# A four-layer trunk: the MLP's input at other offsets, logits in other ticks, a rebuilt start

## The chip, the cores and the metric

The kernel is one launch on one core of a Trainium2 chip. The metric is device time in microseconds (us), taken as the median of several executions. Five engines matter here: PE (TensorE) multiplies matrices and transposes, ACT (ScalarE) and DVE (VectorE) work elementwise, POOL (GpSimd) does small work, SP (SyncE) issues DMAs. They run side by side and meet through semaphores. SBUF is the on-chip memory that PE reads; PSUM has eight banks per partition that PE writes.

## The reference, cut to what matters

```python
D_MODEL, SEQ, DEPTH, D_FF = 1024, 256, 4, 4096     # batch 1, float32
for i in range(DEPTH):
    kind = i % 3            # 0 retention (layers 0 and 3), 1 MoBA attention, 2 differential attention
    h = rmsnorm(x, norm1[i])
    x = x + mixer[kind](h)  # retention: 4 heads, q and k of 256 with rotary, v and gate of 512
                            # attention: 16 heads of 64, q and k normed per head, a T5 bias added
    x = x + square(relu(rmsnorm(x, norm2[i]) @ w_up[i])) @ w_down[i]
return x
```

At 256 tokens the MoBA layer has one block only, so it is plain causal attention. Layers 0 and 3 are retention, layer 1 is MoBA, layer 2 is differential attention.

## The kernel before, in words

**Three passes.** Every float32 operand of a large product is cut in two parts: hi (rounded to the matmul's input format, made by an ACT copy) and lo (the rest, made by a DVE subtraction). `passes` (L310 to L313) then makes three matmuls: hi times hi (L311), one mixed (L312), the other mixed (L313). The activations' parts are `xhi`, `xlo`, the weights' are `whi`, `wlo`.

**Weights.** They stream through SBUF: SP loads `raw` tiles of 1 MB (three buffers) by `load_raw`, each tile is cut into two pieces, `split_piece` (ACT, L173) and `split_lo` (DVE, L183) make the two parts of a piece; `advance` does so up to four pieces ahead of the matmuls, `take` hands a piece out. A matmul takes one operand as "weights", loaded into the array ahead of it (PEld), and streams the other one, the "moving" one. In `mm_a` (q and k of retention: tile `qk`; the MLP's first product: tile `up`) the model weights are loaded and the activations move, 256 columns at a time. In `mm_b` (`vg`, `qkv`) and `mm_o` (`acc`) the activations are loaded and the model weights move, 512 columns at a time.

**Offsets.** `hi_lo` (L86) gives `wlo` a pad of 32 or 96 floats, by the piece's parity, and by whether the piece is narrow (256 columns wide). `norm_new` (L271) lays out `xhi` and `xlo` with pads of 80 and 48 floats, and shifts them for the MLP. What counts in this case is the address modulo 512 bytes: all `whi` lie at 160; `wlo` lies at 32 for narrow pieces and at 160 for wide ones; the MLP's `xhi` lies at 96 and `xlo` at 352, any other `xhi` and `xlo` at 160. While one matmul streams its moving operand, the next one's weights are loaded. Moving minus loaded is thus 448, 320, 448 bytes in the three passes of `up`, and 0, 128, 0 in those of `qk`.

**Order.** The order on each engine is that of the code. A clock counts ticks: `tick` comes after each step of a large product, `later(n, f)` queues a step for n ticks on, and steps due in the same tick go by the table `ORDER` (L64), the transposes of q and k (`qk_t`) late in it.

**Attention.** Layers 1 and 2 make q, k (two halves `b` of 8 heads each) and v in six blocks of four `mm_b`, one tick each. `qk_t` transposes a half to `qT`, `kT` (PE, then ACT copies), `softmax` (L632) makes logits of one pair of heads (PE, tile `sc`, two PSUM banks), adds the bias and takes the maximum (DVE, L651), and exponentiates (ACT, L654); `probs`, `probs_t` and `av_moba` or `av_diff` follow a few ticks later. V is copied from PSUM by ACT (L761, tile `vt`); `av_moba` (tile `oT`) and `av_diff` (tile `od`) need it. Four auxiliary PSUM banks go round among `sc`, `pT`, `qkT`, `oT`, `od`, `up`, `qk`. The table `SM0` (L590) sets the ticks of the softmaxes of the half b = 0 (12 to 15) and of b = 1 (20, 20, 21, 21); k of the half b = 1 is transposed in tick 19.

**Start.** X comes in four transfers of 256 KB, the first weights in two halves, `cos`, `sin` and the decay tables (`kd`, L427) in one transfer that ACT issues. `norm_quarter` (L280) transposes X and makes `xhi` and `xlo` a half of the features at a time; the first 1/rms (`rms`, L295) follows three ticks later.

Of the kernel before, what the change touches and what calls it, by code (L numbers as in the profile page):

```python
# [31 lines left out]
def trunk(ctx, tc, x_in, rel_bias, norm1, norm2, w_up, w_down, ret_w_in, ret_w_out,  # L32
# [108 lines left out]
    raws, pieces = {}, {}  # L141
    nxt = [0, 0, 0, 0]

    def load_raw(half=None):
        i = nxt[0]
        if i >= len(specs):
            return
        src, a, b = specs[i]
        if half != 1:
            raws[i] = rp.tile([P, a, b], F32, tag="raw", name="raw", bufs=NRAW)  # L150
        if half is None:
            nc.sync.dma_start(raws[i], src)
        else:
            hs = slice(half * (a // 2), (half + 1) * (a // 2))
            nc.sync.dma_start(raws[i][:, hs, :], src[:, hs, :])
        if half != 0:
# [68 lines left out]
    POOL.dma_start(rows2[0:32, :], norm2.rearrange("l (c p) -> (l c) p", p=P))
    for i, w in enumerate((moba_q_norm, moba_k_norm, diff_q_norm, diff_k_norm)):
        for g in range(2):
            POOL.dma_start(rows2[32 + i:33 + i, g * HD:(g + 1) * HD], w)
    POOL.dma_start(rows2[36:37, :], diff_subln)
# [193 lines left out]

    def retention(l):
        OT = {}
        kd = mp.tile([P, 8, S], F32, tag="kd", name="kd")
        ACT.dma_start(kd[:, 0:6, :], c_rd.rearrange("a p s -> p a s"))  # L427
        cos_b = kd[:, 0:1, :].to_broadcast([P, 2, S])
        sin_b = kd[:, 1:2, :].to_broadcast([P, 2, S])

# [140 lines left out]
    def attention(l):  # L571
# [8 lines left out]
        def at(tk, fn, *a):  # L580
            later(max(t0 + 1 + tk - clock[0], 0), fn, *a)
# [189 lines left out]
    for t in range(2):
        norm_quarter(0, 0, 0, t)
    split_piece()
    split_lo()
    for t in range(2):
        later(1, norm_quarter, 0, 0, 1, t)
    later(1, split_piece)
    later(1, split_lo)
# [51 lines left out]
```

## Time and profile before

| | |
|---|---|
| median of 3 executions | 1351.65 us (1350.81 to 1352.14) |
| the profiled execution's own time | 1352.26 us |
| its span, first to last instruction | 1350.4 us |
| mean granted TensorE clock | 0.998 |
| PE, DVE, ACT, POOL busy | 99%, 62%, 51%, 8% of the span |
| DMA | 242.27 MB, mean 179 GB/s |
| chain that ended last | PE 97%, ACT 1%, DMA 1% |

A time line row gives the start in us from the span's first instruction, the duration, the engine and line, the tiles, and in brackets how long the engine was idle before and what released it. Matmuls overlap: a row's duration runs to the modelled end of the matmul, so the pace of PE is read from the differences of starts.

### The profile page before, as it was taken

The page shows a single profiled execution, that of the slowest core. Times are in us where ns is not written, and L with a number is a line of the kernel's source. Part 1 is how long each engine was busy: PE and PEld are TensorE (multiplying, and loading weights), DVE is VectorE, ACT ScalarE, POOL GpSimd, SP SyncE. Part 2 cuts the span into 40 slices and gives each one's busy share as a digit, 9 for nine tenths or more (in the row PEclk, how much of TensorE's full clock was granted, in tenths as well). Part 3 has the DMA queues.
Part 4 walks back from the last instruction along what each step waited for, and adds up shares of the span by engine and source line. Part 5 has one row for each costly group of instructions (what it writes and reads, how often), then busy time and mean ns, then how long its engine had stood idle before and what let it go on. Part 6 is the DMA issues. An engine that isn't in the chain of part 4 may idle for free.

```text
span 1350.4 us, 19806 instructions
## 1 busy us (share of the span) xinstructions
PE 1333.6 (99%) x8020; PEld 1170.5 (87%) x8020; DVE 840.6 (62%) x1238; ACT 689.3 (51%) x1063; POOL 106.6 (8%) x314
## 2 busy tenths in 40 slices
PE   7999999999999999999999999999999999999998
PEld 6888889999987779999987789999988888899997
DVE  6766647555568856555578576555667675565554
ACT  5544446444456746444466754444455444554442
POOL 3111100000022000000021110000031011000000
PEclk9999999999999999999999999999999999999999
DMA  8545455555565336555554346555564555465551
GB/s 275 182 162 176 167 196 180 188 187 191 194 210 187 125 125 222 188 188 187 188 176 135 125 140 230 193 187 187 177 205 143 185 171 187 149 225 198 194 187 63
DMA packets 140797, 242.27 MB, mean 179 GB/s; under 512 B 4256, under 2 KB 87920, under 8 KB 140704
## 3 DMA queue, kind: packets, MB, share of 16 engines
q1 hardware_dynamic: 137872, 236.99, 52.3%
q0 software_dynamic: 1072, 2.35, 0.6%
q10 hardware_dynamic: 1760, 1.66, 0.4%
q8 instruction: 63, 1.03, 0.3%
q14 instruction: 30, 0.25, 0.1%
HBM read 239.91 MB, written 1.07 MB: 178 GB/s over the span
## 4 chain that ended last, share of the span: by engine, by line
PE 97%; ACT 1%; DMA 1%; DVE 0%; issue 0%; SPq 0%; ACTq 0%; DVEq 0%
PE acc L311 12%; PE acc L312 12%; PE acc L313 12%; PE up L312 9%; PE up L313 9%; PE up L311 9%; PE vg L311 4%; PE vg L313 4%; PE vg L312 4%; PE qkv L311 3%; PE qkv L313 3%; PE qkv L312 3%; PE qk L313 2%; PE qk L311 2%; PE qk L312 2%; PE xt L286 1%
## 5 line engine op out<-in xcount | busy, mean ns | idle before, releaser
L183 DVE TENSOR_TENSOR wlo<-raw,whi 128x1024 fp32r<-128x1024 f32 (+1 forms) x449 | 529.4, 1219 | 107.9 <-ACT whi L173 100.1
L173 ACT ACTIVATE whi<-raw 128x1024 fp32r<-128x1024 f32 (+1 forms) x449 | 451.8, 1051 | 89.7 <-PE acc L313 66.4
L311 PE MATMUL up<-xhi,whi 128*128 128x256 f32 x1024 | 283.8, 277 | 0.0
L312 PE MATMUL up<-xlo,whi 128*128 128x256 f32 x1024 | 283.5, 277 | 0.0
L313 PE MATMUL up<-xhi,wlo 128*128 128x256 f32 x1024 | 283.2, 277 | 0.0
L311 PE MATMUL acc<-whi,uu 128*128 128x512 f32 x512 | 199.9, 391 | 0.0
L312 PE MATMUL acc<-wlo,uu 128*128 128x512 f32 x512 | 199.6, 390 | 0.0
L313 PE MATMUL acc<-whi,uu 128*128 128x512 f32 x512 | 199.5, 390 | 0.0
L312 PEld LDWEIGHTS up<-xlo,whi 128*128 128x128 f32 x1024 | 192.3, 188 | 2.2
L311 PEld LDWEIGHTS up<-xhi,whi 128*128 128x128 f32 x1024 | 192.2, 188 | 2.2
L313 PEld LDWEIGHTS up<-xhi,wlo 128*128 128x128 f32 x1024 | 192.5, 188 | 0.0
L392 DVE SCALAR_TENSOR_TENSOR u<-up,u 128x512 f32<-128x512 f32 x64 | 44.2, 691 | 203.7 <-ACT u L391 203.5
L391 ACT ACTIVATE u<-up 128x512 f32<-128x512 f32 x64 | 38.1, 595 | 240.9 <-PE up L313 240.9
L313 PEld LDWEIGHTS acc<-whi,uu 128*128 128x128 f32 x512 | 96.1, 188 | 20.2
L311 PEld LDWEIGHTS acc<-whi,uu 128*128 128x128 f32 x512 | 96.1, 188 | 17.8
L312 PEld LDWEIGHTS acc<-wlo,uu 128*128 128x128 f32 x512 | 96.1, 188 | 17.7
L311 PE MATMUL vg<-whi,xhi 128*128 128x512 f32 x256 | 100.5, 393 | 0.0
L313 PE MATMUL vg<-whi,xlo 128*128 128x512 f32 x256 | 99.8, 390 | 0.0
L312 PE MATMUL vg<-wlo,xhi 128*128 128x512 f32 x256 | 99.7, 389 | 0.0
L311 PE MATMUL qkv<-whi,xhi 128*128 128x512 f32 x192 | 78.6, 409 | 0.0
L311 PE MATMUL acc<-whi,oh 128*128 128x512 f32 x192 | 76.5, 398 | 0.0
L313 PE MATMUL qkv<-whi,xlo 128*128 128x512 f32 x192 | 75.7, 394 | 0.0
(212 smaller groups left out, 1803.1 us busy)
## 6 DMA issues: line engine op xcount, KB each, us to landing
raw<-in_w_up_dram SPq DMA_DIRECT2D x64, 1024.0 KB, 5.6
raw<-in_w_down_dram SPq DMA_DIRECT2D x64, 1024.0 KB, 5.9
raw<-in_ret_w_in_dram SPq DMA_DIRECT2D x47, 1024.0 KB, 5.2
raw<-in_ret_w_out_dram SPq DMA_DIRECT2D x16, 1024.0 KB, 4.8
raw<-in_moba_w_in_dram SPq DMA_DIRECT2D x12, 1024.0 KB, 5.2
raw<-in_diff_w_in_dram SPq DMA_DIRECT2D x12, 1024.0 KB, 5.1
raw<-in_moba_w_out_dram SPq DMA_DIRECT2D x4, 1024.0 KB, 4.9
raw<-in_diff_w_out_dram SPq DMA_DIRECT2D x4, 1024.0 KB, 5.1
```

The source lines that it names most:

```text
L173: ACT.activation(hi[:, part], half[:, part], AF.Copy)
L183: DVE.tensor_tensor(lo[:, part], half[:, part], hi[:, part].bitcast(F32), op=OP.subtract)
L286: PE.transpose(ps[:, i * P:(i + 1) * P], X[:, t, k * P:(k + 1) * P], ident)
L311: PE.matmul(ps, lhsT=ah, rhs=bh, start=first, stop=False, skip_group_check=True)
L312: PE.matmul(ps, lhsT=ah, rhs=bl, start=False, stop=False, skip_group_check=True)
L313: PE.matmul(ps, lhsT=al, rhs=bh, start=False, stop=last, skip_group_check=True)
L391: ACT.activation(u, ps, AF.Relu)
L392: DVE.scalar_tensor_tensor(u, ps, 0.0, u, op0=OP.max, op1=OP.mult)
```

## The change

**Offsets.** `hi_lo` loses its pads, so every part of the weights lies at 160 modulo 512. `norm_new` shifts both parts of the MLP's input by one number of floats, `SHIFT`, that differs by layer: moving minus loaded weights is 448, 352, 320 and 192 bytes in layers 0, 1, 2 and 3, the same in all three passes. Other activations stay at 160, so all three passes of `qk` are at distance 0. The 512-column products keep their distance.

**Logits.** `SM0` lists a tick for each softmax. Those of b = 1 move from ticks 20, 20, 21, 21 to 19, 19, 20, 21, in layers 1 and 2. Two of the four thus follow the transposes of k directly.

**Start.** X comes in four column quarters, the first weights in parts of two k, alternating on SP, and `cos`, `sin` and the decay come on SP too. Nine matmuls on zeroed bf16 data (`hot`) stand ahead on PE. `first_qk` transposes, splits and multiplies two k at a time. POOL's small loads wait for tick 4, `head_weights` goes from tick 10 to 14. Pieces up to the fourth are split in two halves.

```diff
@@ hi_lo
-        n = a * b
-        hi = wp.tile([P, n], F32R, tag="hi", name="whi", bufs=NPC)
-        odd = i % 2
-        lo = wp.tile([P, n + (32 if odd else 96)], F32R, tag="lo%d" % (i % NPC), name="wlo", bufs=1)
-        o = 0 if odd == narrow else (32 if odd else 96)
-        return (t.rearrange("p (a b) -> p a b", a=a) for t in (hi, lo[:, o:o + n]))
+        return (wp.tile([P, a, b], F32R, tag=t, name="w" + t, bufs=NPC) for t in ("hi", "lo"))
@@ parts
-        m = n if i else n // 2
+        m = n if i > 3 else n // 2
@@ the first loads
-    ACT.dma_start(ident, c_ident)
-    nc.sync.dma_start(X[:, 0, 0:512], xf[0:P, 0:512])
-    ACT.dma_start(rows, norm1.rearrange("l (c p) -> (l c) p", p=P))
-    nc.sync.dma_start(X[:, 1, 0:512], xf[P:S, 0:512])
+    ACT.dma_start(rows, norm1.rearrange("l (c p) -> (l c) p", p=P))
+    nc.sync.dma_start(X[:, :, 0:S], xv[:, :, 0:S])
+    ACT.dma_start(ident, c_ident)
+    load_raw(0, 4)
     ACT.activation(warm, warm, AF.Copy)
-    load_raw(0)
-    for t in range(2):
-        nc.sync.dma_start(X[:, t, 512:D], xf[t * P:(t + 1) * P, 512:D])
-    load_raw(1)
-    for _ in range(1, NRAW):
-        load_raw()
+    for i in range(1, 4):
+        nc.sync.dma_start(X[:, :, i * S:(i + 1) * S], xv[:, :, i * S:(i + 1) * S])
+        load_raw(i, 4)
+    load_raw(0, 2)
+    nc.sync.dma_start(kd0[:, 0:2, :], rd[:, 0:2, :])
+    load_raw(1, 2)
+    for i in range(2):
+        load_raw(i, 2)
+    nc.sync.dma_start(kd0[:, 2:6, :], rd[:, 2:6, :])
+    hot = aux_bank("hot")
+    for _ in range(9):
+        PE.matmul(hot, lhsT=junk[:, :P], rhs=junk[:, :512], start=True, stop=True)
@@ norm_new
-        lo = xp.tile([P, n + 48], F32R, tag="xlo", name="xlo")
-        hi = xp.tile([P, n + 80], F32R, tag="xhi", name="xhi")
-        oh, ol = (64, 48) if mlp_in else (80, 0)
+    SHIFT = (112, 88, 80, 48)
+        o = 0 if mlp_layer is None else SHIFT[mlp_layer]
+        for part in ("hi", "lo"):
+            x = xp.tile([P, n + 128], F32R, tag="x" + part, name="x" + part)
+            st[part] = x[:, o:o + n].rearrange("p (k s) -> p k s", k=KC)
@@ first_qk (new)
+        def turn(pr):
+...
+            ACT.activation(hi[:, kk], raw, AF.Copy)
+            DVE.tensor_tensor(lo[:, kk], raw, hi[:, kk].bitcast(F32), op=OP.subtract)
+        def meet(pr):
+...
+        turn(0)
+        turn(1)
+        for pr in range(4):
+            meet(pr)
+            if pr < 2:
+                turn(pr + 2)
+            if pr == 2:
+                nxt[1] = nxt[2] = nxt[3] = 2
+                load_raw()
+                for _ in range(2):
+                    split_piece()
+                    split_lo()
+            if pr:
+                tick()
@@ attention
-        SM0, AV0 = (12, 20), (20, 24)
+        SM0, AV0 = ((12, 13, 14, 15), (19, 19, 20, 21)), (20, 24)
-                    at(SM0[b] + (i // 2 if b else i), softmax, b, i)
+                    at(SM0[b][i], softmax, b, i)
@@ the end of trunk
-    later(10, head_weights)
+    later(4, small_loads)
+    later(14, head_weights)
```

The order on ACT at the start, from the first `xhi` on (`whi` are weight pieces, `junk,ss` the squares for the first 1/rms). Before:

```order
L289 ACTIVATE xhi<-xt,W 128x128 x8
L173 ACTIVATE whi<-raw 128x512 x2
L427 DMA kd<-in_c_rd_dram 128x6x256
L289 ACTIVATE xhi<-xt,W 128x128 x8
L173 ACTIVATE whi<-raw 128x1024 x5
L298 ACTIVATE junk,ss<-X 128x1024 x2
```

After:

```order
L351 ACTIVATE xhi<-xt,W 128x256 x2
L359 ACTIVATE whi<-raw 128x512
L351 ACTIVATE xhi<-xt,W 128x256 x2
L359 ACTIVATE whi<-raw 128x512
L351 ACTIVATE xhi<-xt,W 128x256 x2
L359 ACTIVATE whi<-raw 128x512
L351 ACTIVATE xhi<-xt,W 128x256 x2
L359 ACTIVATE whi<-raw 128x512
L163 ACTIVATE whi<-raw 128x512 x4
L305 ACTIVATE junk,ss<-X 128x1024 x2
L163 ACTIVATE whi<-raw 128x1024 x6
```

Four steps of two `xhi` and one `whi` stand where two larger ones stood, and two whole pieces fewer are split ahead of the squares.

The order on DVE around the first rotary (`ra` to `qk`). Before:

```order
L183 TENSOR_TENSOR wlo<-raw,whi 128x1024 x5
L303 RECIPROCAL r_272<-me 128x2
L435 TENSOR_TENSOR ra<-qk,kd 128x512
L436 TENSOR_TENSOR rb__290<-qk,kd 128x512
L437 TENSOR_TENSOR qk<-ra,rb__290 128x256
L438 TENSOR_TENSOR qk<-rb__290,ra 128x256
L183 TENSOR_TENSOR wlo<-raw,whi 128x1024 x2
```

After:

```order
L173 TENSOR_TENSOR wlo<-raw,whi 128x512 x4
L310 RECIPROCAL r_254<-me 128x2
L506 TENSOR_TENSOR ra<-qk,kd 128x512
L507 TENSOR_TENSOR rb__272<-qk,kd 128x512
L508 TENSOR_TENSOR qk<-ra,rb__272 128x256
L509 TENSOR_TENSOR qk<-rb__272,ra 128x256
L173 TENSOR_TENSOR wlo<-raw,whi 128x1024 x4
```

The lo parts of the pieces 4 and 5, which the first `vg` products read, moved behind the reciprocal and the rotary.

The order on ACT in layer 1 from the copies of k of b = 1 on. Before:

```order
L627 ACTIVATE kT<-qkT,W 128x4x128 x2
L173 ACTIVATE whi<-raw 128x1024
L761 ACTIVATE vt<-qkv,r 128x512 x2
L703 ACTIVATE oh<-oT 128x256
L654 ACTIVATE e,sm<-e,nm 128x128 x2
L654 ACTIVATE e,sm<-e,nm 128x256 x2
```

After:

```order
L701 ACTIVATE kT<-qkT,W 128x4x128 x2
L728 ACTIVATE e,sm<-e,nm 128x128 x2
L728 ACTIVATE e,sm<-e,nm 128x256 x2
L728 ACTIVATE e,sm<-e,nm 128x128 x2
L728 ACTIVATE e,sm<-e,nm 128x256 x2
L163 ACTIVATE whi<-raw 128x1024
L835 ACTIVATE vt<-qkv,r 128x512 x2
L777 ACTIVATE oh<-oT 128x256
```

The eight exponentials of two softmaxes moved ahead of a weight piece and of the two copies of V. On PE the eight logits matmuls of these two softmaxes moved from behind the first `oT` to right behind the transposes of k, and on DVE their maxima moved ahead of one `wlo`.

## Rows read from the trace of the kernel before

**Rows 1.** page, part 1: busy time, share of the span, instructions.

```profile
PE 1333.6 (99%) x8020; PEld 1170.5 (87%) x8020; DVE 840.6 (62%) x1238; ACT 689.3 (51%) x1063; POOL 106.6 (8%) x314
```

**Rows 2.** PE groups by shape: busy us, mean ns of one | idle.

```profile
L311 PE MATMUL up<-xhi,whi 128*128 128x256 f32 x1024 | 283.8, 277 | 0.0
...
L311 PE MATMUL qk<-xhi,whi 128*128 128x256 f32 x256 | 73.5, 287 | 2.1 <-ACT whi L173 2.1
L313 PE MATMUL qk<-xhi,wlo 128*128 128x256 f32 x256 | 72.8, 284 | 0.8 <-DVE wlo L183 0.8
```

**Rows 3.** PE timeline, layer 0's MLP: start, us, instruction [idle before].

```profile
215.09 0.28 PE L312 MATMUL up<-xlo,whi 128*128 128x256 f32 x1
...
216.56 0.28 PE L313 MATMUL up<-xhi,wlo 128*128 128x256 f32 x1
```

**Rows 4.** timeline of PE over the first 32 us.

```profile
4.92 0.28 PE L233 MATMUL wps<-ident,rows 32*128 32x32 f32 x1 [4.92 <-DMA rows<-in_norm_dram]
...
9.25 0.58 PE L311 MATMUL qk<-xhi,whi 128*128 128x256 f32 x1 [2.15 <-ACT whi L173]
...
11.42 0.41 PE L313 MATMUL qk<-xhi,wlo 128*128 128x256 f32 x1
...
19.84 0.28 PE L311 MATMUL qk<-xhi,whi 128*128 128x256 f32 x1
...
25.55 0.40 PE L311 MATMUL vg<-whi,xhi 128*128 128x512 f32 x1
```

**Rows 5.** timelines of ACT, then DVE, over the first 32 us.

```profile
5.86 2.17 ACT L289 ACTIVATE xhi<-xt,W 128x128 fp32r<-128x128 f32 x8 [2.69 <-PE xt L286]
8.56 0.63 ACT L173 ACTIVATE whi<-raw 128x512 fp32r<-128x512 f32 x1 [0.54 <-DMA raw<-in_ret_w_in_dram]
...
21.74 1.04 ACT L298 ACTIVATE junk<-X 128x1024 bf16<-128x1024 f32 x1
...
26.44 2.35 DVE L183 TENSOR_TENSOR wlo<-raw,whi 128x1024 fp32r<-128x1024 f32 x2
```

**Rows 6.** timelines of PE, ACT, DVE in layer 1, second half of the attention.

```profile
450.15 0.48 PE L311 MATMUL qkv<-whi,xhi 128*128 128x512 f32 x1
...
453.30 1.06 PE L698 MATMUL oT<-pT,vt 128*64 128x256 f32 x8 [0.16 <-ACT vt L761]
454.29 1.93 PE L644 MATMUL sc<-kT,qT 64*128 64x128 f32 x16
...
462.65 0.50 PE L311 MATMUL qkv<-whi,xhi 128*128 128x512 f32 x1
...
452.56 1.31 ACT L761 ACTIVATE vt<-qkv,r 128x512 f32<-128x512 f32 x2 [0.35 <-PE qkv L313]
...
459.11 1.04 ACT L173 ACTIVATE whi<-raw 128x1024 fp32r<-128x1024 f32 x1
...
451.55 0.55 DVE L686 COPY pT<-pT 128x384 f32<-128x384 f32 x1
452.01 2.35 DVE L183 TENSOR_TENSOR wlo<-raw,whi 128x1024 fp32r<-128x1024 f32 x2
...
455.25 0.29 DVE L651 CUSTOM_DVE_ANT_0 e<-sc,bt 128x128 f32<-128x128 f32 x1
```

**Rows 7.** timelines of PE, then DVE, at the same place in layer 2.

```profile
745.08 0.49 PE L717 MATMUL od<-vt,pT 128*128 128x128 f32 x2 [0.16 <-ACT vt L761]
...
750.00 1.26 PE L644 MATMUL sc<-kT,qT 64*128 64x128 f32 x8 [0.94 <-DVE nm L651]
...
756.59 1.27 PE L644 MATMUL sc<-kT,qT 64*128 64x128 f32 x8 [1.53 <-DVE nm L651]
757.78 0.60 PE L311 MATMUL qkv<-whi,xhi 128*128 128x512 f32 x1
...
741.07 4.62 DVE L183 TENSOR_TENSOR wlo<-raw,whi 128x1024 fp32r<-128x1024 f32 x4
```

**Rows 8.** busy time by engine (x instructions), PEclk, DMA; layer 2.

```profile
758.00:762.00 4.00, 4.00 (x12) 3.09 (x12) 3.86 (x15) 3.76 (x10) 0.78 (x3) 0.57 0.01 4
```

More of the change, by code (lines that the diff above doesn't have):

```diff
@@ L142, in trunk, with load_raw @@
     nxt = [0, 0, 0, 0]
-    def load_raw(half=None):
+    def load_raw(part=0, of=1):
         i = nxt[0]
@@ L148, in load_raw @@
         src, a, b = specs[i]
-        if half != 1:
+        if part == 0:
             raws[i] = rp.tile([P, a, b], F32, tag="raw", name="raw", bufs=NRAW)
[L151 to L156, printed above, removed]
+        hs = slice(part * (a // of), (part + 1) * (a // of))
+        nc.sync.dma_start(raws[i][:, hs, :], src[:, hs, :])
+        if part == of - 1:
             nxt[0] += 1
     def parts(i, n):
-        m = n if i else n // 2
+        m = n if i > 3 else n // 2
         return [slice(c, c + m) for c in range(0, n, m)]
@@ L208, in trunk @@
     warm = const.tile([P, 1], F32, name="warm")
+    junk = const.tile([P, D], mybir.dt.bfloat16, name="junk")
+    kd0 = mp.tile([P, 8, S], F32, tag="kd", name="kd")
+    rd = c_rd.rearrange("a p s -> p a s")
+    pad8 = mp.tile([P, 8], F32, name="pad8")
+    nc.vector.memset(pad8, 0.0)
+    DVE.memset(junk, 0.0)
     DVE.memset(warm, 0.0)
+    xv = xf.rearrange("(t p) d -> p t d", p=P)
+    ACT.dma_start(rows, norm1.rearrange("l (c p) -> (l c) p", p=P))
+    nc.sync.dma_start(X[:, :, 0:S], xv[:, :, 0:S])
@@ L221, in trunk @@
+    load_raw(0, 2)
[7 more added lines that the diff above has]
+        PE.matmul(hot, lhsT=junk[:, :P], rhs=junk[:, :512], start=True, stop=True)
     rb = const.tile([NB_REL, AH], F32, name="rb")
-    POOL.dma_start(rb, rel_bias)
     rows2 = mp.tile([64, P], F32, tag="t2k", name="rows2", bufs=4)
-    POOL.memset(rows2, 0.0)
@@ L225, in trunk, with small_loads @@
[L225 to L229, printed above, removed]
+    def small_loads():
+        POOL.dma_start(rb, rel_bias)
+        POOL.memset(rows2, 0.0)
+        POOL.dma_start(rows2[0:32, :], norm2.rearrange("l (c p) -> (l c) p", p=P))
+        for i, w in enumerate((moba_q_norm, moba_k_norm, diff_q_norm, diff_k_norm)):
+            for g in range(2):
+                POOL.dma_start(rows2[32 + i:33 + i, g * HD:(g + 1) * HD], w)
+        POOL.dma_start(rows2[36:37, :], diff_subln)
@@ L265, in rsqrt, with norm_new @@
                 eng.tensor_tensor(y, t, y, op=OP.mult)
-    junk = const.tile([P, D], mybir.dt.bfloat16, name="junk")
     st = {}
-    def norm_new(mlp_in=False):
+    SHIFT = (112, 88, 80, 48)
+    def norm_new(mlp_layer=None):
         n = KC * S
-        lo = xp.tile([P, n + 48], F32R, tag="xlo", name="xlo")
-        hi = xp.tile([P, n + 80], F32R, tag="xhi", name="xhi")
-        oh, ol = (64, 48) if mlp_in else (80, 0)
-        st["hi"] = hi[:, oh:oh + n].rearrange("p (k s) -> p k s", k=KC)
-        st["lo"] = lo[:, ol:ol + n].rearrange("p (k s) -> p k s", k=KC)
+        o = 0 if mlp_layer is None else SHIFT[mlp_layer]
+        for part in ("hi", "lo"):
+            x = xp.tile([P, n + 128], F32R, tag="x" + part, name="x" + part)
+            st[part] = x[:, o:o + n].rearrange("p (k s) -> p k s", k=KC)
     def norm_quarter(l, which, c, t):
@@ L327, in mm_a, with first_qk @@
         tick()
+    def first_qk(ps):
+        for i in range(2):
+            pieces[i] = tuple(hi_lo(i, 4, S, True))
+        def turn(pr):
+            bank = aux_bank("xt")
+            for i in range(2):
+                for t in range(2):
+                    c0 = i * S + t * P
+                    k = 2 * pr + i
+                    PE.transpose(bank[:, c0:c0 + P], X[:, t, k * P:(k + 1) * P], ident)
+            for i in range(2):
+                k = 2 * pr + i
+                ACT.activation(st["hi"][:, k, :], bank[:, i * S:(i + 1) * S], AF.Copy, scale=wn(0, 0, k))
+            for i in range(2):
+                k = 2 * pr + i
+                DVE.scalar_tensor_tensor(st["lo"][:, k, :], bank[:, i * S:(i + 1) * S], wn(0, 0, k),
+                                         st["hi"][:, k, :].bitcast(F32), op0=OP.mult, op1=OP.subtract)
+            hi, lo = pieces[pr // 2]
+            kk = slice(pr % 2 * 2, pr % 2 * 2 + 2)
+            raw = raws[0][:, 2 * pr:2 * pr + 2, :]
+            ACT.activation(hi[:, kk], raw, AF.Copy)
+            DVE.tensor_tensor(lo[:, kk], raw, hi[:, kk].bitcast(F32), op=OP.subtract)
+        def meet(pr):
+            ks = (2 * pr, 2 * pr + 1)
+            hi, lo = pieces[pr // 2]
+            for k in ks:
+                for m in range(2):
+                    mc = slice(m * P, (m + 1) * P)
+                    pc = ps[:, m * S:(m + 1) * S]
+                    PE.matmul(pc, lhsT=hi[:, k % 4, mc], rhs=st["hi"][:, k, :], start=k == 0 and m == 0, stop=False,
+                              skip_group_check=True)
+                    PE.matmul(pc, lhsT=hi[:, k % 4, mc], rhs=st["lo"][:, k, :], start=False, stop=False,
+                              skip_group_check=True)
+            for k in ks:
+                for m in range(2):
+                    mc = slice(m * P, (m + 1) * P)
+                    PE.matmul(ps[:, m * S:(m + 1) * S], lhsT=lo[:, k % 4, mc], rhs=st["hi"][:, k, :], start=False,
+                              stop=k == KC - 1 and m == 1, skip_group_check=True)
+        turn(0)
[12 more added lines that the diff above has]
+                tick()
+        for i in range(2):
+            pieces.pop(i)
@@ L365, in finish @@
         if nxt_norm is not None:
-            norm_new(nxt_norm[1] == 1)
+            norm_new(nxt_norm[0] if nxt_norm[1] == 1 else None)
         for q in QUARTERS:
@@ L425, in retention @@
         OT = {}
-        kd = mp.tile([P, 8, S], F32, tag="kd", name="kd")
-        ACT.dma_start(kd[:, 0:6, :], c_rd.rearrange("a p s -> p a s"))
+        if l == 0:
+            kd = kd0
+        else:
+            kd = mp.tile([P, 8, S], F32, tag="kd", name="kd")
+            ACT.dma_start(kd[:, 0:6, :], rd)
         cos_b = kd[:, 0:1, :].to_broadcast([P, 2, S])
@@ L507, in retention @@
                 ps = aux_bank("qk")
-                mm_a(ps, 0, h == 0 and w == 0)
-                mm_a(ps, 1)
+                if l == 0 and h == 0 and w == 0:
+                    first_qk(ps)
+                else:
+                    mm_a(ps, 0, h == 0 and w == 0)
+                    mm_a(ps, 1)
                 rotary(ps, qk[:, 2 * w:2 * w + 2, :])
@@ L770, in trunk @@
     norm_new()
[L771 to L778, printed above, removed]
     later(3, rms, 0)
-    later(10, head_weights)
+    later(4, small_loads)
+    later(14, head_weights)
     for l in range(DEPTH):
```

## The prediction

> **What bounds the kernel now.** I read the page first: PE is busy 99% of the span [rows 1], so a gain has to come from one of three things: a faster pace of matmuls that follow each other, a stretch at the lower clock, or one of the few microseconds in which PE stands still. Then I read PE's groups by shape, for the pace; then PE's timeline with the idle time in brackets, for the stops; and beside each stop the timelines of ACT and DVE, for what ends last there.
>
> Pace: 13 matmuls of `up` go from 215.09 to 216.56, one per 113 ns [rows 3], and the 3072 of them last 277 ns on average (a row runs to the end of the pipeline, so that differences between rows count, not the length). `qk` has the same shape and lasts 287 and 284 ns [rows 2]. What differs is the distance modulo 512 bytes between moving and loaded operand: 448, 320, 448 in `up`, 0, 128, 0 in `qk`.
>
> Stops: at the start PE waits 4.92 us for the first small loads and 2.15 us for the first weight piece, the first group of 96 `qk` matmuls lasts until 19.84, and the second until 25.55, where `vg` begins [rows 4]. [...]
>
> **Start.** The first piece comes at 8.56 on ACT, released by a DMA [rows 5], with 512 KB of X and 512 KB of weights ahead. Now 256 KB of each stand ahead, so I put the first `xhi` at about 6.3 (an estimate: after the 4.92 of the first loads, and before 8.56). One step of two k on ACT is two `xhi` of 256 columns and one `whi` of 0.63 us [rows 5]. 128 columns take 2.17 / 8 = 0.27 [rows 5], so I take 0.4 for 256, and 1.45 for a step. Four steps and a little waiting for weights end at 12.7. Four half pieces at 0.63 follow, then the squares at 15.2, where they stood at 21.74. From the start of the squares to the first `wlo` behind the rotary it is 26.44 - 21.74 = 4.70 us now [rows 5]. That `wlo` belongs to piece 4 in the new order, and the second matmul of `vg` reads it: 15.2 + 4.7 + 2.35 / 2 = 21.1. PE is there earlier: its first group can end at about 14.0, the second takes 25.55 - 19.84 = 5.71, so 19.7. So `vg` runs from 21.1 instead of 25.55, a gain of 4.4; I give 0.1 back at the first scores, since DVE is now late by that much with its rotary. I take **-4.3**. What is late next is thus DVE, with the pieces that moved behind the rotary, and no longer the DMA. Bounds: without DVE's lateness PE alone would give 25.55 - 19.7 = 5.9. The other end is PE at the lower clock. The first nine `qk` matmuls last 0.41 each at the pace of 0.21, later ones 0.28 [rows 4]; at 0.21 a step of 12 matmuls takes 2.6 us instead of 1.4 and the first group would end near 18, which leaves 25.55 - 23.7 = 1.9. The nine `hot` matmuls stand against that; their own time lies within the 4.92 us in which PE waits anyway. POOL's small loads move behind the squares, off everyone's way; if `head_weights` had to wait for them at tick 14, a PE transpose would, and I see no row that says so.
>
> **Logits in layer 1.** PE leaves the transposes of k at 450.15 [rows 6]. Of the four auxiliary banks the second one that the new logits take is that of a `pT` which DVE copies at 451.55 for 0.55 us [rows 6]. So the two moved softmaxes run from 452.1, with 1.93 us for two [rows 6], to about 453.95 (a stop of some 1.5 us that wasn't there). The twelve `qkv` matmuls behind take 453.30 - 0.16 - 450.15 = 2.99 and end at 456.95. Meanwhile DVE does one `wlo` to 452.01 + 1.18 = 453.2, then the maxima; from the first maximum to the last exponential it is 459.11 - 455.25 = 3.86 now [rows 6], so ACT is free at 457.05, makes a weight piece (1.04) until 458.1, and only then the copies of V, 1.31 for both [rows 6]: 458.75 and 459.4. The copies stood at 452.56 before, ahead of the exponentials. `oT` waits for them, so that PE stops from 456.95 to 458.75. Behind it `oT` ends at 459.8, one softmax takes 0.97, the next `qkv` 2.99, `oT` and one softmax 1.8: the last `qkv` block begins at 465.5, where it began at 462.65 [rows 6]. I take **+2.7**, with 0 and +3.5 as ends: 0 if the scheduler of banks and the copies run as before, +3.5 if the second half of V holds the whole of `oT`.
>
> **Logits in layer 2.** The same chain: three `wlo` end at 741.07 + 3 x 1.155 = 744.5 [rows 7], + 3.86 + 1.04 = 749.4, the first V copy at 750.1. `od` began at 745.08 and now begins 5.0 later, a stop of 2.8. But what stood between 745.08 and 757.78 gets shorter: the stops of 0.94 and 1.53 go, with some 0.3 of restart each, as do the logits of two softmaxes, 1.93, which have gone ahead. 12.70 - 2.47 - 0.6 - 1.93 = 7.7, so 757.8 against 757.78 [rows 7]: **0**. The stretch at half clock lay behind two stops; now one stop of 2.8 us stands in layer 2, and stops of 1.5 and 1.8 in layer 1, which look like the 0.94 and 1.53 of before. I keep one stretch of 1.7 us in the sum, as before; none gives -1.7, two give +1.7.
>
> **Offsets in `qk`.** All three passes go to distance 0, where two of three were. The pass whose loads lay at 128 moves to 0. If that pass had been the good one, and drew its neighbours with it, the pace gets worse by at most what the mean now stands above `up`: 768 x 7 to 10 ns, so +5.4 at the outside; if 0 throughout is as good as 448 the same amount is won, less the start's share, -4.8. The rows nearest to it are the 512-column products, which are at distance 0 already, but with twice the time per load. I take +0.5, as the two kinds of pass lie within 3 ns of each other.
>
> **Offsets in `up`.** `up` runs at 113 ns at 448 and 320, so it can win little: 1 ns off the mean of 277 in all 3072 would be 3 us, and I allow no more than 2. It can lose: a layer whose new distance behaved like that of `qk` would take 768 x 7 ns = 5.4 us more. Layer 0 keeps 448, which is seen in two passes of three. 352 (layer 1) lies between 320 and 448. 320 (layer 2) is seen in one pass. 192 (layer 3) is in no row, nearest to 128 on one side and 320 on the other. I take +0.3 for all four.
>
> [...] By rows, the length differs between two groups of the same shape, 277 against 284 to 287 [rows 2]. [...]
>
> **The sum.** -4.3 + 2.7 + 0 + 0.5 + 0.3 = -0.8. Against the profiled execution's own 1352.26 that is 1351.5; the median lies 0.6 lower, so 1350.9, and I say **1351.0**. A measurement of this kernel can tell about 0.2%, 2.7 us, from no change, so the forecast is "the same": what the start wins the logits of layer 1 mostly give back.
>
> **Rivals.** (1) Faster: the V copies are not late, and no stretch of half clock is left. Then the layer 1 term is +1.0 instead of 2.7 and -1.7 is added: -4.3 + 1.0 - 1.7 + 0.8 = -4.2, so 1347; with the start at its bound 5.9 it is 1345.5, and a `qk` that reaches 277 gives as much. For it: ACT is only half busy [rows 1]. Against it: ACT takes its work in order, and the copies stand behind eight exponentials. (2) Slower: one MLP distance falls out of the pace of 113 ns, 192 in layer 3 or 352 in layer 1. It decides from 5 ns per matmul, 3.8 us in one layer; at 7 ns it is 1351 + 5.4 = 1356.4, and 1361.8 for two layers. For it: `qk` is out at 0 and 128. Against it: two distances far apart, 320 and 448, are both in pace. (3) No distance matters: what `qk` has more than `up` comes from its place in the program, among transposes and first loads, and the terms 0.5 and 0.3 go, 1350.2, within the same 0.2%. For it: `qk` holds the start with its half clock. Against it: the start is one group of sixteen, and 7 ns in all of them is more. (4) The half clock comes in both attention layers and PE is cold at the start: -1.9 + 2.7 + 1.7 + 0.8 = +3.3, 1354.3.
>
> **How the numbers follow.** Forecast 0.25 and rival (3) 0.15, both within 0.2%: 0.40. Rival (1) and its kin, from -2.7 on: 0.33. Rival (2): 0.15. Rival (4): 0.12. So faster 0.33, same 0.40, slower 0.27. The range leaves out two MLP layers out of pace and everything beyond the best start: 1345.5 to 1357.0. The cases within 0.2% alone span 1349 to 1354.
>
> **What the profile would show.** The start is right if `vg` begins near 21 behind a `wlo`, and wrong if it begins behind a DMA or PE lasts 0.41 per `qk` matmul throughout. Layer 1 is right if PE stops before `oT`, released by `vt`; layer 2 if the stops before `sc` are gone and one before `od` stands there. PEclk below 1 in either tells of the 1.7. The means of `up` layer by layer tell of each distance, that of `qk` of 0 throughout. The prediction fails if any of these means moves by over 3 ns, or if the copies of V come earlier than I worked out.

## The result, and the profile after

The changed kernel takes 1363.36 us (1362.72 to 1364.72) against 1351.79 us: ratio 1.0089, interval 1.0077 to 1.0102. It is slower by 11.6 us; 1351.0 was predicted, with 1345.5 to 1357.0 as range. The profiled execution took 1362.72 us, its span is 1360.9 us, 10.5 more than before.

Where the time went, by the start of each stage's first PE matmul in the two traces:

| stage | begins, before | after minus before | the stage's own part |
|---|---|---|---|
| `vg`, layer 0 | 25.55 | -4.9 | start -4.9 |
| MLP, layer 0 | 209.55 | -3.8 | +1.1 |
| layer 1 | 387.19 | -1.5 | MLP of layer 0 **+2.3** |
| MLP, layer 1 | 503.58 | +0.7 | attention of layer 1 **+2.2** |
| layer 2 | 680.30 | +5.8 | MLP of layer 1 **+5.0** |
| MLP, layer 2 | 798.16 | +4.9 | attention of layer 2 **-0.8** |
| layer 3 | 974.87 | +8.2 | MLP of layer 2 **+3.3** |
| MLP, layer 3 | 1170.53 | +8.2 | retention of layer 3 0.0 |
| end | 1345.74 | +10.5 | MLP of layer 3 **+2.3** |

The page's first part and PE's groups by shape (busy us, mean ns of one | idle before):

```profile
PE 1347.6 (99%) x8029; PEld 1182.5 (87%) x8029; DVE 840.4 (62%) x1235; ACT 688.1 (51%) x1058; POOL 109.6 (8%) x314
```

```profile
L318 PE MATMUL up<-xhi,whi 128*128 128x256 f32 x1024 | 288.4, 282 | 0.0
L319 PE MATMUL up<-xlo,whi 128*128 128x256 f32 x1024 | 287.5, 281 | 0.0
L320 PE MATMUL up<-xhi,wlo 128*128 128x256 f32 x1024 | 287.3, 281 | 0.0
...
L318 PE MATMUL qk<-xhi,whi 128*128 128x256 f32 x240 | 68.6, 286 | 0.0
L320 PE MATMUL qk<-xhi,wlo 128*128 128x256 f32 x240 | 67.9, 283 | 0.0
```

PE is still busy 99%, as in [rows 1], but 14 us more: `up` has gone from 277 ns [rows 2] to 281 and 282, with no idle time before it. `qk` has hardly moved (286 and 283 against 287 and 284). The middle pass of `up` by layer, the same view over the four MLPs in turn:

```profile
L319 PE MATMUL up<-xlo,whi 128*128 128x256 f32 x256 | 71.8, 281 | 0.0
```

```profile
L319 PE MATMUL up<-xlo,whi 128*128 128x256 f32 x256 | 72.3, 283 | 0.0
```

```profile
L319 PE MATMUL up<-xlo,whi 128*128 128x256 f32 x256 | 71.5, 279 | 0.0
```

Layer 3 reads as layer 0 does. All four layers are out of pace, layer 0 too, at the distance 448 that two passes of three had before. Layers 0 and 3 are not out from their start, though. Two stretches of layer 0's `up`, from the second and from the third of its sixteen groups of 48 matmuls:

```profile
214.23 0.28 PE L318 MATMUL up<-xhi,whi 128*128 128x256 f32 x1
...
215.48 0.28 PE L320 MATMUL up<-xhi,wlo 128*128 128x256 f32 x1
```

```profile
225.22 0.28 PE L318 MATMUL up<-xhi,whi 128*128 128x256 f32 x1
...
226.51 0.28 PE L320 MATMUL up<-xhi,wlo 128*128 128x256 f32 x1
```

11 matmuls take 1.25 us, then 1.29. In layers 0 and 3 the first two groups go at 113.4 ns and the other fourteen at 117.8, with the same offsets. PE's waits (total us, times, longest):

```profile
PE oT L772 <- ACT vt L835: 2.7, 1, 2.7
PE od L791 <- ACT vt L835: 2.6, 1, 2.6
...
PE sc L718 <- ACT kT L701: 0.7, 2, 0.3
...
PE vg L319 <- DVE wlo L173: 0.2, 1, 0.2
```

The stops before the logits that DVE's maxima ended are gone, two short ones for `kT` are left, and two stops for the copies of V stand there instead. The start, by the timelines of PE, ACT and DVE, which answer to [rows 4, 5]:

```profile
1.49 4.02 PE L225 MATMUL hot<-junk 128*128 128x512 bf16 x9 [1.49 <-DVE warm L205]
...
7.87 0.39 PE L370 MATMUL qk<-xhi,whi 128*128 128x256 f32 x1 [0.35 <-ACT whi L359]
...
14.92 0.28 PE L318 MATMUL qk<-xhi,whi 128*128 128x256 f32 x1
...
27.17 1.55 PE L517 MATMUL s<-qk 128*128 128x256 f32 x8 [0.38 <-DVE qk L508]
```

```profile
15.28 1.05 ACT L305 ACTIVATE junk<-X 128x1024 bf16<-128x1024 f32 x1
```

```profile
19.99 2.35 DVE L173 TENSOR_TENSOR wlo<-raw,whi 128x1024 fp32r<-128x1024 f32 x2
```

The first `qk` matmul lasts 0.39 and the next ones 0.28, where matmuls still lasted 0.41 at 11.42 before. By these lengths PE is at its full pace at 8 us. The record of the granted clock begins at 5.70 us in this trace and at 13.93 in the one before, with 1.00 each time, so that no clock stands on record for the slow matmuls, and no run takes out the `hot` ones by themselves. The second group begins at 14.92 instead of 19.84. Then layer 1, which answers to [rows 6], and layer 2, to [rows 7, 8]; the last row is a stretch of layer 2, with the granted clock, 0.72, behind the busy times:

```profile
449.24 2.35 PE L718 MATMUL sc<-kT,qT 64*128 64x128 f32 x16 [0.34 <-ACT kT L701]
451.52 0.50 PE L318 MATMUL qkv<-whi,xhi 128*128 128x512 f32 x1
...
457.19 1.01 PE L772 MATMUL oT<-pT,vt 128*64 128x256 f32 x8 [2.65 <-ACT vt L835]
...
463.61 0.50 PE L318 MATMUL qkv<-whi,xhi 128*128 128x512 f32 x1
```

```profile
455.52 1.04 ACT L163 ACTIVATE whi<-raw 128x1024 fp32r<-128x1024 f32 x1
456.47 1.24 ACT L835 ACTIVATE vt<-qkv,r 128x512 f32<-128x512 f32 x2
```

```profile
755.74 0.49 PE L791 MATMUL od<-vt,pT 128*128 128x128 f32 x2 [2.55 <-ACT vt L835]
```

```profile
755.00:761.00 6.00, 5.26 (x32) 4.98 (x32) 1.23 (x1) 3.16 (x14) 0.00 (x0) 0.72 0.54 175
```

PE stops 2.65 us in layer 1 and 2.55 in layer 2, until ACT has copied V, and in layer 2 a stretch at the lower clock follows ((1 - 0.72) x 6.00 = 1.7 us, where before [rows 8] give (1 - 0.57) x 4.00 = 1.7).

### The profile page after: what moved, and what is told of

It reads as the page before. It is cut to its first block, busy times and chain, and to the rows that moved or that the text cites. A ratio compares the mean times of both kernels' runs of the same rounds, so it can differ in the third digit from the quotient of the medians.

```text
span 1360.9 us, 19835 instructions
## 1 busy us (share of the span) xinstructions
PE 1347.6 (99%) x8029; PEld 1182.5 (87%) x8029; DVE 840.4 (62%) x1235; ACT 688.1 (51%) x1058; POOL 109.6 (8%) x314
## 4 chain that ended last, share of the span: by engine, by line
PE 93%; DVE 3%; ACT 2%; DMA 1%; issue 1%; DVEq 0%; ACTq 0%
PE acc L318 12%; PE acc L320 12%; PE acc L319 12%; PE up L318 9%; PE up L320 9%; PE up L319 9%; PE vg L318 4%; PE vg L320 4%; PE vg L319 4%; PE qkv L318 2%; PE qkv L320 2%; PE qkv L319 2%; PE qk L318 2%; PE qk L320 2%; PE qk L319 2%; ACT e L728 1%
## 5 line engine op out<-in xcount | busy, mean ns | idle before, releaser
L318 PE MATMUL up<-xhi,whi 128*128 128x256 f32 x1024 | 288.4, 282 | 0.0
L319 PE MATMUL up<-xlo,whi 128*128 128x256 f32 x1024 | 287.5, 281 | 0.0
L320 PE MATMUL up<-xhi,wlo 128*128 128x256 f32 x1024 | 287.3, 281 | 0.0
```

Source lines behind the costliest of these rows:

```text
L318: PE.matmul(ps, lhsT=ah, rhs=bh, start=first, stop=False, skip_group_check=True)
L319: PE.matmul(ps, lhsT=ah, rhs=bl, start=False, stop=False, skip_group_check=True)
L320: PE.matmul(ps, lhsT=al, rhs=bh, start=False, stop=last, skip_group_check=True)
```

## The experiments

**The offsets, taken out and put in alone.** e1 is the changed kernel with `hi_lo` and `norm_new` of before, e2 the kernel before with those of the change (the two hunks of the diff above, backwards and forwards).

> The changed kernel with the offsets of the kernel before (both weights' parts and the MLP's input); start and logits stay changed. The two traces put +2.3, +5.0, +3.3 and +2.3 us of the result into the four MLPs, 12.9 in all. Theory A, the offsets alone do that: up goes back to a mean of 277 ns in all layers and the time falls to about 1363.4 - 12.9 = 1350.5 us. Rival B, what moves the pace is the start or the logits (another phase of the streams): up stays at 281 to 282 ns and the time near 1363.

Measured: 1349.22 us, ratio 0.9986 (0.9977 to 0.9995). `up` is back at 277 ns, and each MLP takes what it took before:

```profile
L324 PE MATMUL up<-xlo,whi 128*128 128x256 f32 x1024 | 283.5, 277 | 0.0
```

> The kernel before with nothing but the new offsets. Theory A: up at 281 to 282 ns, time 1351.8 + 12.9 = 1364.7 us, with qk at 0.0 to +0.3 us against before. Rival B: up at 277 ns, time within 1 us of before.

Measured: 1364.85 us, ratio 1.0100 (1.0085 to 1.0116); `up` at 281, and `qk` 0.25 us slower in each of the two retention layers:

```profile
L307 PE MATMUL up<-xlo,whi 128*128 128x256 f32 x1024 | 287.3, 281 | 0.0
```

Theory A stands, rival B falls: the offsets cost more than the whole difference, and the rest of the change gains.

**Which offset.** e3 gives each layer's `up` its own arrangement:

```diff
+    W32 = (False, True, False, True)
...
-        hi, lo = hi_lo(i, a // 2, b, a == 8)
+        hi, lo = hi_lo(i, a // 2, b, W32[up_layer[r]] if r in up_layer else a == 8)
...
+    SHIFT_HI, SHIFT_LO = (112, 112, 112, 112), (48, 112, 16, 80)
```

> The kernel before with another arrangement of up in each layer; start, logits and qk as before. xhi stays at 96 and whi at 160. Layer 0: xlo 352, wlo 160, so that the moving operand jumps by 256 between the passes and the loaded weights do not jump, distances 448, 192, 448. Layer 1: xlo 96, wlo 32, moving steady and weights jumping, distances 448, 64, 448. Layer 2: xlo 224, wlo 160, moving jumps, weights steady, again 448, 64, 448. Layer 3: xlo 480, wlo 32, both jump, but the distance is 448 throughout. Theory A1, what costs is one common distance in all passes: layers 0 to 2 at the pace of before (mean start to start 114.2 ns), layer 3 at 117 to 118. Theory A2, the moving operand must jump: layers 0, 2, 3 at 114.2, layer 1 at 117 or more. Theory A3, wlo must lie at 32, off whi: layers 1 and 3 at 114.2, layers 0 and 2 at 117 or more.

Measured in a single run: 1362.23 us. The same row of `up` for the four MLPs in turn:

```profile
L315 PE MATMUL up<-xlo,whi 128*128 128x256 f32 x256 | 71.8, 280 | 0.0
```

```profile
L315 PE MATMUL up<-xlo,whi 128*128 128x256 f32 x256 | 70.9, 277 | 0.0
```

```profile
L315 PE MATMUL up<-xlo,whi 128*128 128x256 f32 x256 | 72.3, 282 | 0.0
```

```profile
L315 PE MATMUL up<-xlo,whi 128*128 128x256 f32 x256 | 73.4, 287 | 0.0
```

Start to start the means are 117.5, 114.2, 118.0 and 121.1 ns. All three theories fall: layers 1 and 2 had the same three distances (448, 64, 448) and differ, so A1 falls, and with it any rule by which the pace goes by those distances; layers 0 and 2 jump and are slow, so A2 falls; layer 3 had `wlo` at 32 and is the slowest, so A3 falls as it stood. So I made a map. e5, e6 and e7 set the input by layer and `wlo` by groups of `up` within a layer:

```diff
+        if w is not None:
+            o = W_AT[w][odd]
...
+    W_AT = ((0, 32), (32, 0), (64, 0), (96, 0))
...
+    SHIFT_HI, SHIFT_LO = (16, 48, 80, 96), (16, 48, 80, 96)
```

(This is e7; e5 has 112, 0, 64, 32 for both, e6 112 throughout for `xhi` and 0, 32, 64, 96 for `xlo`.)

> The kernel before; only addresses in up change. Both parts of the input lie at one place per layer, xhi = xlo = whi + 448, 0, 256, 128 bytes in layers 0 to 3; within each layer, wlo lies at whi + 0, 128, 256, 384 in four groups of up each (for 128 and 256 in the first half of a group only, its second half has 384). Theory C, wlo must lie off whi and nothing else counts: 113 to 115 ns per matmul wherever it does, 117 to 120 where wlo = whi, in all layers. Theory D, the three distances between moving and loaded operand must differ, whichever they are: the same as C here. Theory E, only some places of the input do, 448 with wlo at 384 as in layer 1 of the third experiment: layer 0 at 384 has 114, layer 1 (input at 0, as in qk) stays at 119 to 120 for all four.

> The kernel before; in up xhi stays at whi + 448, xlo lies at whi + 0, 128, 256, 384 in layers 0 to 3, wlo in each layer at whi + 0, 128, 256, 384 by groups of four. Theory C: slow (117 to 122) for wlo = whi only. Theory D: slow also where xlo - wlo = 448, which none of these has, so fast in all where wlo is off whi. Theory E: wlo at 384 is fast with xlo at some places (192 and 448 were fast, 320 slow), and the map shows which.

> As e5, with the input at whi + 64, 192, 320, 384 in layers 0 to 3. Theories C and D: fast wherever wlo is off whi. Theory E: fast at 384 only for inputs near 448.

Measured in single runs: 1365.05, 1363.72 and 1364.31 us. Mean start to start in ns of the first half of a group of `up`, from its seventh matmul on, for `xhi` = `xlo` (e5 and e7; a row is the input's distance from `whi`, a column that of `wlo`, both in bytes modulo 512; the first column leaves out a layer's first two groups):

| input | wlo +0 | +128 | +256 | +384 |
|---|---|---|---|---|
| 0 | 120.0 | 119.3 | 120.0 | 119.4 |
| 256 | 120.0 | 119.3 | 120.0 | 119.4 |
| 64 | 117.7 | 119.0 | 117.8 | 119.0 |
| 320 | 117.7 | 119.0 | 117.8 | 119.0 |
| 128 | 119.9 | 118.4 | 119.9 | 118.4 |
| 384 | 119.9 | 118.4 | 119.9 | 118.4 |
| 192 | 117.7 | **113.3** | 117.7 | **113.3** |
| 448 | 117.7 | **113.3** | 117.8 | **113.3** |

(A layer's first group is broken up by transposes. At 448 with `wlo` at +0 the second ran at 113.4, as in layers 0 and 3 of the changed kernel; in e7's layer 1, at 192 with `wlo` at +0, it ran at 117.8. So in that place one and the same arrangement has two paces, and its addresses don't settle which; what does isn't shown. Where `wlo` is at +128 or +384 every group holds 113.3.) The rows pair off, and so do the columns: what lies 256 bytes further agrees within 0.1 ns. Only one cell in the reduced table is fast throughout, at 113.3: input 192 modulo 256 above `whi`, and `wlo` 128 modulo 256 off `whi`. In e6, with `xhi` at 448, no place of `xlo` of the four is fast, 117.8 to 120.0 (read as in the table). Theories C and D fall; E is right, but with places that repeat after 256 bytes in these maps. In the trace of e7 the pace changes within layer 1 from one group of `up` to the next, where `wlo` goes from +0 to +128:

```profile
539.82 0.28 PE L316 MATMUL up<-xhi,whi 128*128 128x256 f32 x1
...
541.12 0.28 PE L318 MATMUL up<-xhi,wlo 128*128 128x256 f32 x1
```

```profile
548.07 0.28 PE L316 MATMUL up<-xhi,whi 128*128 128x256 f32 x1
...
549.31 0.28 PE L318 MATMUL up<-xhi,wlo 128*128 128x256 f32 x1
```

11 matmuls in 1.30 us are 118 ns each; 11 in 1.24 are 113. This reading, theory P from here on, sorts all that came before. The kernel before had `xhi` at 448, `xlo` at 192 and `wlo` at 384 from `whi`: three distances, but modulo 256 one common input place of 192 and 128 for `wlo`. Layer 1 of e3 is the same cell. The change took `wlo` to +0 in all layers, and moved the input off 192 in layers 1 (96) and 2 (64). To test it, e10 puts `wlo` back and nothing else:

```diff
+        for t, o in (("hi", 0), ("lo", 32)):
+            w = wp.tile([P, n + (64 if o else 0)], F32R, tag=t, name="w" + t, bufs=NPC)
+            o = o if narrow else 0
...
```

> The changed kernel with one thing put back: wlo of the narrow pieces lies 128 bytes off whi (128 modulo 256), the input stays at whi + 448, 352, 320, 192 by layer. Theory P: layers 0 and 3 (both 192 modulo 256) fall to 114.2 ns, layer 2 (64) goes to 119, layer 1 (96) to between 118 and 120, so -2.5, -1 , +0.7, -2.5 us: about 1358 us. Rival, the input's common place is what costs: layers 0 and 3 stay at 117.5 and the time at 1363.

Measured: 1360.08 us, ratio 1.0062 (1.0048 to 1.0076). By MLP:

```profile
L323 PE MATMUL up<-xlo,whi 128*128 128x256 f32 x256 | 70.9, 277 | 0.0
```

```profile
L323 PE MATMUL up<-xlo,whi 128*128 128x256 f32 x256 | 73.3, 286 | 0.0
```

```profile
L323 PE MATMUL up<-xlo,whi 128*128 128x256 f32 x256 | 72.4, 283 | 0.0
```

Layer 3 reads as layer 0 does: both are at 114.2 ns, at distances 192 and 448, as P says; layer 2 is at 119.2. Layer 1, at the place 96 that the map lacks, went up to 121.1 instead of down (1.6 us above my figure), and its attention met a stretch at the lower clock (granted 0.78 from 452 to 458 us and 0.94 from 458 to 464, so (1 - 0.78) x 6.00 + (1 - 0.94) x 6.00 = 1.7 us); less small gains elsewhere, these two make up the 2 us by which the time is above it. In layers 1 and 2 the input's new places are thus enough by themselves to cost the pace.

**Start and logits.** e4 is e1 with the ticks of before.

> The changed kernel with the offsets and the ticks of the logits of the kernel before, so that the new start alone is left. By the traces the start is 3.8 us ahead when the output product of layer 0 begins: 1351.8 - 3.8 = 1348.0 us. If the lead is lost later (a lead of DMA or of pieces that shrinks), 1350 to 1352. Against e1 this prices the logits: +2.2 in layer 1 and -0.8 in layer 2, so e1 1.4 us above it.

Measured: 1346.64 us, ratio 0.9970 (0.9960 to 0.9981). The start gains 4.3 us in its trace and keeps it to the end; the trace ends 6.1 ahead, as its layer 2 met no stretch at the lower clock (granted 1.00 from 730 to 775 us). By the medians e1 is 2.6 us above e4. In the traces the new ticks cost +2.2 in layer 1 and -0.7 in layer 2, and 1.0 of e1's 2.5 lies in layer 0 already, where the two run the same code: `vg` begins at 22.05 in e1 and at 21.00 in e4. A start of this kind is thus known to about 1 us from one trace. Two runs ask what makes V late. e11 (on e9, below) moves one softmax of layer 1, not two: `SM0` (19, 20, 20, 21).

> e9 with one softmax of layer 1 in tick 19 instead of none (ticks 19, 20, 20, 21). My reading of the stop at oT: the V copies stand behind the exponentials that have gone ahead, eight in the changed kernel, four here, so the copies come some 1.75 us earlier and the stop shrinks from 2.7 to about 0.9 us; against e9 layer 1 loses that, and wins back the stop of 0.75 before the logits of tick 21: 0 to +1 us in layer 1. Rival, the stop comes from the wait for the PSUM banks or from the weight piece ahead of the copies: it stays at 2 us or more.

Measured: 1344.53 us against e9's 1343.81; in layer 1 the trace is 1.4 us behind e9's. The stop is 1.9 us:

```profile
PE oT L771 <- ACT vt L834: 1.9, 1, 1.9
```

```profile
449.47 1.04 ACT L167 ACTIVATE whi<-raw 128x1024 fp32r<-128x1024 f32 x1
450.42 1.24 ACT L834 ACTIVATE vt<-qkv,r 128x512 f32<-128x512 f32 x2
```

The copies did come earlier, by the 1.8 us that I had worked out: 6.8 us after the transposes of k begin (443.62) instead of 8.6 (447.87 to 456.47, in the changed kernel). But PE comes to them earlier too, by the 0.97 of the second softmax's logits: I had left that out, and 2.65 - 1.8 + 0.97 is 1.8. The rival's 2 us or more are so near that e11 alone does not settle it. e12 keeps both softmaxes in tick 19, and issues their exponentials a tick later, behind the copies:

```diff
...
+            if b == 1 and i < 2:
+                later(1, exps)
+            else:
+                exps()
```

> e9 with the changed kernel's ticks of the logits (19, 19, 20, 21) in both attention layers, but the exponentials of the two softmaxes of tick 19 issued one tick later, behind the copies of V; their logits and maxima stay in tick 19. My reading, the copies of V are late because the exponentials stand ahead of them on ACT: the stops of 2.7 us before oT and 2.6 before od shrink to under 0.5, as do those before the logits of ticks 20 and 21 (the maxima still free the banks early). Against e9 layer 1 goes by -0.5 to 0 us, layer 2 by -2 us; time 1343.8 - 2 = 1341.8. Rival, something else releases the copies late (the weight piece ahead of them, DVE): the stops stay over 2 us, and layer 1 stands 2 us above e9.

Measured: 1347.85 us, ratio 0.9974 (0.9964 to 0.9983). PE's waits:

```profile
PE pT L762 <- ACT pT L767: 2.0, 4, 0.6
...
PE pT L762 <- DVE e L749: 1.2, 2, 0.9
PE oT L828 <- DVE on L822: 1.1, 1, 1.1
...
PE oT L781 <- ACT vt L844: 0.2, 1, 0.2
```

The stop before `oT` is 0.2, that before `od` is no longer listed: the exponentials ahead of the copies were the cause (the weight piece behind them, 1.0 us, was held up with the copies, and goes ahead now). But the probabilities come later now, and PE waits 2.0 and 1.2 us at their transposes (`pT`) and 1.1 at `oT` of layer 2; layers 1 and 2 lose 1.8 and 1.9 us against e9, where I had put -0.5 to 0 and -2. The stop has been moved, not removed.

**A version that beats both.** e8 has `wlo` as before, the MLP's input and the retention layers' input both at `whi` + 448, has the new start, and the new ticks in layer 2 alone. e9 reaches the same places with the weights instead, and leaves all activations at 160:

```diff
+        for t, o in (("hi", 16), ("lo", 48)):
+            w = wp.tile([P, n + 64], F32R, tag=t, name="w" + t, bufs=NPC)
+            o = o if narrow else 0
...
```

> The new start; the new ticks of the logits in layer 2 alone, the old ones in layer 1; wlo of narrow pieces at 32 as before; and both parts of the input at 96, whi + 448, for the MLPs and for the retention layers' own input too, so that qk gets the arrangement that held 114.2 ns in up. From e4's 1346.6: layer 2's logits -0.8, qk 768 x 6 ns = -4.6, so 1341. If the place of the input costs vg what qk wins (there it is the loaded side, now 64 bytes off the moving one), 1346 or more. If qk does not lock in the place where up does, because of the work around it, 1345.5.

> The rule that the maps give, made with the weights alone: all activations stay at 160, narrow whi move by 64 bytes, narrow wlo by 192, so that in qk and up the moving operand is 192 modulo 256 above whi, and wlo 128 modulo 256 off whi; wide pieces, and with them vg, qkv and acc, keep their distance of 0 modulo 256. Half of the tiles lie 256 bytes further by their buffer. New start, new ticks of the logits in layer 2 alone. Theory P, a period of 256 bytes and two conditions: up at a mean of 114.2 ns start to start in all layers though its buffers differ by 256, qk at 114 to 115 in layer 3 instead of 120, vg at 228.4 as before; time e8's 1344.8 less the 1.6 and 0.5 us that vg lost there: 1342 to 1343. Rival, the period is 512 and e7 met its floor by chance: half of the pieces at 117 or more, time above 1350.

Measured: e8 1344.76 us, ratio 0.9951 (0.9937 to 0.9964); e9 1343.81 us, ratio 0.9940 (0.9928 to 0.9953), 8.1 us faster than before. The middle pass of `qk` in layer 3, before, in e8 and in e9, and `vg` in e8:

```profile
L312 PE MATMUL qk<-xlo,whi 128*128 128x256 f32 x128 | 36.1, 282 | 0.0
```

```profile
L321 PE MATMUL qk<-xlo,whi 128*128 128x256 f32 x128 | 35.4, 277 | 0.0
...
L321 PE MATMUL vg<-wlo,xhi 128*128 128x512 f32 x128 | 50.3, 393 | 0.0
```

```profile
L318 PE MATMUL qk<-xlo,whi 128*128 128x256 f32 x128 | 35.4, 276 | 0.0
```

`qk` falls from 282 to 277 and 276: start to start, the 384 of a layer take 1.8 (layer 0) and 2.0 us (layer 3) less in e9 than in e4, 3.8 for the 4.6 that I had put there. The middle pass of `vg` of layer 3 is at 393 in e8, with its loaded side moved (390 before), and `vg` costs 0.5 us more there; in e9, where it stays, it is back at 390. In layer 0 `vg` takes 1.2 (e8) and 1.3 us (e9) more than in e4, PE's stops for DVE counted in. In e9 the stops are all of it (0.9 before the first scores, where e4 has none, and 0.5 before `vg`'s second matmul for 0.2); in e8 they are 0.5, and what is left is near the cost in layer 3. So I had blamed the addresses for stops in part. Most of the rest of e8's miss of 3.8 us is the lower clock, which its layer 2 meets behind the stop before `od` (granted 0.66 from 745 to 750 us, (1 - 0.66) x 5.00 = 1.7). The rival of e9, a period of 512, falls: half its tiles lie 256 bytes further, and `up` holds 114.0 ns in all layers.

## Why the prediction was wrong, step by step

**Offsets in `up`: the step that failed.** I costed it at +0.3 for all four layers; it measured +2.3, +5.0, +3.3 and +2.3, 12.9 us. The prediction argued pass by pass: a pass's pace belongs to its own distance modulo 512 between the moving and the loaded operand, so 448 and 320, seen at 113 ns, were safe wherever they stand. Neither half holds. In the maps places 256 bytes apart agree within 0.1 ns, and e9 holds 114.0 with half its tiles 256 bytes further, so that `xhi` at 448 and `xlo` at 192 from `whi` were one place before, and the distances had to be taken modulo 256, not 512; and the pace belongs to the whole arrangement of the three passes, `wlo` against `whi` among it: layers 1 and 2 of e3 have the same three distances and run at 114.2 and 118.0 ns. I read the removal of the pad in `hi_lo` as part of "one common distance", and never priced it by itself; e10 shows that it alone takes layers 0 and 3 from 277 to 281. In layers 1 and 2 the input's places, 352 and 320, fail as well.

**Rival (2)** gave the side and the engine, and nearly the size (5.4 us a layer, where 2.3 to 5.0 were measured). Of the two distances that it named, 352 in layer 1 was the worst, but 192 in layer 3 is as good as 448; all layers failed at once, 0 and 3 by the pad of `wlo`, which it did not name. That shared cause is what the range lacked: it left out two layers, and four came. **Rival (3)**, that no distance matters, falls with e2 and the map: with nothing but addresses edited, equal work on equal shapes ran at 113.3 to 121 ns. Why the places have this effect isn't shown by any run here.

**Offsets in `qk`:** +0.5 predicted, +0.5 measured (e2, 0.25 in each layer).

**Start:** -4.3 predicted, -4.9 at `vg`, -3.8 by the layer's output, -4.3 there in e4. What ends last was named rightly and timed well: squares at 15.2 against 15.28, the `wlo` behind the rotary at 19.9 against 19.99, the matmul that reads it at 21.1 against 21.26. PE came to `vg` a microsecond later than worked out, 20.67 for 19.7, so that it stopped for that `wlo` for 0.2 only. Of the 1.1 us that the changed kernel loses again by the end of the layer's mixer, 0.6 are this stop and one of 0.38 before the first scores, where the prediction had 0.1, and 0.2 are the offsets in `qk`; e4 lacks the second stop and loses 0.3. That PE's slow pace at the start, 0.21 us from start to start, is the lower clock (the bound of 1.9, rivals (3) and (4)) was my reading, and the record of the clock doesn't reach there; it is near what the trace before shows where the clock does read 0.50: `qkv` matmuls start at 758.61 and 759.04, 0.43 apart, and at 762.22 and 762.45, 0.23 apart, at 1.00.

**Logits, layer 1:** +2.7 predicted, +2.2 measured, by the stop that was named (2.65 us before `oT`, released by `vt`). V came when worked out: `oT` begins at 457.19, and since the layer starts 1.5 earlier than before, that is 458.7 for 458.75. The first stop, before the logits, was 0.34 and some 0.4 inside the sixteen matmuls for 1.5, so that PE only came earlier and waited longer, 2.65 for 1.8. The 0.5 lies behind `oT`: the last `qkv` block begins at 463.61, which is 465.1 for 465.5. **Layer 2:** 0 predicted, -0.8 measured, stop of 2.55 for 2.8. **The clock:** one stretch kept, one measured. The 1.7 us by which the prediction and its rivals (1) and (4) count a stretch are those of [rows 8], 0.57 over 4.00 us; in half microseconds the clock reads 0.50 from 758.5 to 761.0 there. e1 has the same stops as the changed kernel and no such stretch (granted 1.00 from 730 to 775 us), so that the count came out right is luck.

Without `up` the sum was thus -1.1, against 10.5 - 12.9 = -2.4 in the trace.

**Slips in the working** that don't bear on the miss: a group of `qk` has 48 matmuls and not 96 (the steps were counted as 4 x 12, rightly); 768 x 7 to 10 ns is 5.4 to 7.7 us and not 5.4 at the outside; rival (4)'s +3.3 counts from the 1351.65 of before and gives 1355.0.

## What to carry to other kernels

Before an address pad is removed, price it as an edit of its own: tabulate the places of all operands of the loop modulo a small power of two (the maps here repeat after 256 bytes), and ask whether each new row was ever seen as a whole, not pass by pass. One run that gives each layer or group another arrangement reads a map off the trace for the price of one; read several groups of each, since one arrangement can show two paces. And a step that is moved ahead in the order of an engine is paid for by what stood behind it (on ACT here, by V's copies: a stop of 2.65 us, and of 0.2 with the copies ahead, e12): look who waits for that.

## What the runs showed of the hardware

The float32 matmuls of 256 columns, with their weights loaded under the matmul ahead (PEld busy 87% of the span beside PE's 99%), ran start to start in 113.3 ns in one arrangement (input 192 modulo 256 above `whi`, `wlo` 128 off `whi`: e5 and e7; 114.2 as the mean of a whole layer in e3 and e10) and, but for one place, in 117.5 to 121.1 in the others that were measured (e3, e5, e6, e7, e10). In e5 to e7 the places of the four operands (`xhi`, `xlo`, `whi`, `wlo`) were all that was edited, and places 256 bytes apart agreed within 0.1 ns (e5, e7); steps finer than 64 bytes for the input (but for the place 96) and than 128 for `wlo` weren't tried. At that one place (input 192 modulo 256, `wlo` +0) both paces were measured in the changed kernel: 113.4 in the first two groups of the MLPs of layers 0 and 3, 117.8 in all later ones. A product of 512 columns reacted less: 393 instead of 390 ns in the middle pass of `vg` when the distance went from 0 to 64 bytes (e8). The lower clock came in layer 2 in some kernels (before, 0.57 over 4.00 us; the changed kernel, 0.72 over 6.00) and not in others with equal stops (e4 and e1, 1.00 from 730 to 775 us), 1.7 us both times that it came, so that a difference of that size in one trace says nothing of an edit.
